# Attention maxima of two heads by pairs of 64-row products, taken in groups of four at the batches of value products

## The chip, the cores and the metric

The kernel runs on one core of one Trainium2 chip. The metric is the device time of one execution in microseconds (us). Five engines work side by side, each through its own list of instructions in order: TensorE (PE: matrix products; PEld is its loading of the stationary operand), VectorE (DVE), ScalarE (ACT), GpSimd (POOL), and SyncE (SP), which issues most DMAs. Products land in PSUM, eight banks of 128 rows by 512 numbers; only DVE and ACT read it here.

## The reference

One layer of a hybrid block over 2048 latent and 256 context tokens. Its first half has two parts that the kernel runs at the same time:

```
s = jnp.einsum('bqkgd,bnkd->bkgqn', q, keys) * scale     # 8 query heads, 2 key heads, head size 64
p = jax.nn.softmax(s, axis=-1)                           # over 2304 keys
o = jnp.einsum('bkgqn,bnkd->bqkgd', p, vals)
...
S_new = exp(b_last) * S + (k * exp(b_last - b))^T v      # gated recurrence, 4 heads, both directions
o = A v + (q * exp(b)) S                                 # A: masked, decayed scores within a chunk
```

Before it come norms and one wide input projection; after it come an output projection and a gated feed-forward layer. The change touches the attention, and two lines of the preparation of its keys.

## The kernel before

**The attention stage.** The work is cut into 32 items: one key head (2) and 128 queries (16), which is four query heads of 128 columns side by side. An item has 18 steps `k`, one for each 128 keys. In a step, `scores` makes one bank `s` of 128 keys by 512 columns with two products (L1190, L1191), and ACT takes its exponential into `p` (L1194). Twice in an item the value products of the steps so far are made in a **batch**: `products` (L1215) and the row sums (L1223). `EVENTS = [10, 20]`: the first batch of an item (eight steps, `av`) is at its own step 10, the second (ten steps) at step 2 of the next item.

**The operands.** A key is kept as a high and a low part of 64 rows each; a tile `K` holds the high parts in rows 0 to 63 and the low parts in rows 64 to 127, and `qa` holds the high part of the queries twice, so that a product over 128 rows adds both parts of the key. `qb` and `KB` (L1191) add the low part of the queries, and take off a maximum.

**The maxima.** The exponential needs, for each query, a bound close to its largest score, before the item starts. So an earlier pass makes the scores the other way round (queries in rows) and keeps only their minimum (signs are turned). `chunk(c)` does a piece: for c under 16, one head and 512 keys (L1159), whose bank `mx` DVE reduces to one column of `mn` (L1161); c = 16 and 17 take the last 256 keys of two heads each (L1165, L1167). After the last one DVE makes `neg` (L1171). At step 10, `maxima` turns it with a transpose `pn` (L1176) and sends it into a row of `qb`. The list `CHUNKS` puts one chunk on each of 18 steps, from step 8 of the item before the last to step 7 of the item before.

**The recurrence** is woven in between. At each batch there is a *round*: products `pa` (L818) for up to two lanes, then `level`, where DVE writes them under a mask into `A` (the copies, L831, one for each lane), ACT moves and POOL multiplies. Transposes `pk` (L889), state products `psf` and `psb` (L902, L922), diagonals `pd` (L804) and readouts `po` (L963 to L965) stand at steps that the tables `KEYS`, `FWD`, `CHAIN`, `DIAG` and `OUT` give; the pattern repeats with each recurrence head, every seven items. `extend` makes the decays `T` on DVE (L873), and the chain of states is carried on DVE from `psb` and `psf` (L943, L915). At step 13 of each item, `finish` makes `pb` (L1239) and DVE scales the item before by it (`oo`, L1241).

**Banks.** PSUM is shared out as `s` 3 banks, `av` 1, `mx` (and `pn`) 2, and `h` 2 for all products of the recurrence and `pb`.

**Order.** In this stage PE, DVE, ACT and POOL each run their instructions in the order in which the program issues them (`manual_schedule`); nothing is moved by a scheduler. In the main loop a step issues its scores, its chunk, work put off by `later`, the recurrence's `step`, `maxima`, `finish`, and at a batch: `pa`, the one sum that DVE adds (L1205), the value products, then `level`.

Of the kernel before, what the change touches and what calls it, by code (L numbers as in the profile page):

```python
# [16 lines left out]
P = 128  # L17
# [19 lines left out]
MLAG = 4  # L37
WL = 1, 3
P5M = False
WOV = (1, 3, 5, 7)  # L40
N_NT = 4
N_S, N_T, N_H = 2, 2, 2
# [25 lines left out]
def block_kernel(ctx: ExitStack, tc: tile.TileContext, a: dict, out: bass.AP, dbg=None):  # L68
# [240 lines left out]
    with proj as st:  # L309
# [223 lines left out]
        def qk_side(t, c):  # L533


            isq = c is not None
            name = f"{'q' if isq else 'k'}{c}_{t}"
            nh = 4 if isq else 2
            n = nh * 64
            lt = t - 2 if t >= 2 else None  # L540
            e = qp.tile([P, 512], F32, tag="qe", name=f"e{name}", bufs=QE)
            raw = e[:, n:2 * n]
            src = s_qraw[c, lt * P:(lt + 1) * P, :] if isq else s_kraw[t * P:(t + 1) * P, :]
            nc.sync.dma_start(raw, src)
# [12 lines left out]
            nc.vector.tensor_tensor(x, hv(raw), rs[:, :, None].to_broadcast([P, nh, 64]), op=ALU.mult)  # L557
            nc.vector.tensor_tensor(x, x, gqk[:, 0 if isq else 1, None, :].to_broadcast([P, nh, 64]),
                                    op=ALU.mult)
            if lt is not None:  # L560
                y = hv(raw)
                y5 = raw.rearrange("p (h g s d) -> p h g s d", g=2, s=2, d=16)
                x5 = e[:, :n].rearrange("p (h g s d) -> p h g s d", g=2, s=2, d=16)
                sn = cs[:, 1, :].rearrange("p (g s d) -> p g s d", g=2, s=2)
                for g in range(2):
                    for s in range(2):
                        nc.vector.tensor_tensor(
                            y5[:, :, g, s, :], x5[:, :, g, 1 - s, :],
                            sn[:, g, s, :][:, None, :].to_broadcast([P, nh, 16]), op=ALU.mult)
# [143 lines left out]
    with ExitStack() as st:  # L713
# [281 lines left out]
        class Recurrence:  # L995
# [112 lines left out]
            def round(self):  # L1108
# [16 lines left out]
                            later(*p[i])  # L1125
                yield

        BATCHES = [[0, 8], [8, 18]]
        ROUNDS = [0, 1]
        EVENTS = [10, 20]  # L1130

        class Item:
# [17 lines left out]

            def chunk(self, c):

                if c == 0:
                    self.mn = sm.tile([P, 4, 5], F32, tag="mn", name=f"mn{self.nm}")
                s = ps_mx.tile([P, 512], F32, tag="x", name=f"mx{self.nm}_{c}")
                K = KS[self.g]
                if c < 16:
                    h, k = divmod(c, 4)
                    nc.tensor.matmul(s, self.qa[:, h * P:(h + 1) * P], K[:, k * 512:(k + 1) * 512],  # L1159
# [2 lines left out]
                else:  # L1162
                    h = (c - 16) * 2
                    for i in range(2):
# [4 lines left out]
                if c == 17:  # L1169
                    self.neg = sm.tile([P, 4], F32, tag="neg", name=f"neg{self.nm}")  # L1170
                    nc.vector.tensor_reduce(self.neg, self.mn, axis=AX.X, op=ALU.min)  # L1171

            def maxima(self):

                pm = ps_mx.tile([P, 512], F32, tag="x", name=f"pn{self.nm}")
                nc.tensor.transpose(pm[:4, :P], self.neg, ident)  # L1176
                mr = sm.tile([4, P], F32R, tag="mr", name=f"mr{self.nm}", bufs=2)
                nc.scalar.activation(mr, pm[:4, :P], AF.Copy)
                for h in range(4):
                    nc.sync.dma_start(f32v(self.qb[64:65, h * P:(h + 1) * P]), f32v(mr[h:h + 1, :]))  # L1180

            def scores(self, k):
# [7 lines left out]
                nc.tensor.matmul(s, KS[self.g][:, ks], self.qa, start=True, stop=False)  # L1190
                nc.tensor.matmul(s, KB[k // 6][:, k % 6 * P:(k % 6 + 1) * P], self.qb,  # L1191
# [55 lines left out]
        KB = [kvp.tile([P, NTOK // 3], F32R, name=f"KB{r}") for r in range(3)]  # L1247
        VS = [kvp.tile([P, 6, 64], F32, name=f"VS{r}") for r in range(3)]
        QB = [qpl.tile([P, 512], F32R, name=f"qb{i}") for i in range(2)]
        one32 = kvp.tile([P, 32], F32, name="one32")  # L1250
        nc.gpsimd.memset(one32, 1.0)
        pick = kvp.tile([P, 2, P], F32, name="pick")
# [8 lines left out]
            nc.sync.dma_start(VS[r], s_v[r * 768:(r + 1) * 768, g * 64:(g + 1) * 64].rearrange("(t p) v -> p t v", p=P))  # L1261

        def load_kb(g, r):
            n = NTOK // 3
            nc.sync.dma_start(f32v(KB[r][:64, :]), s_k[g][:64, r * n:(r + 1) * n])

        for t in QB:
            nc.gpsimd.memset(f32v(t[64:, :]), 0.0)
# [60 lines left out]
        def turn_heads(t, hs, eng, lag=0, ps=ps_h, tag="h"):  # L1329

            pt = ps.tile([P, 512], F32, tag=tag, name=f"mt{t}_{hs[0]}")
            for i, h in enumerate(hs):
                nc.tensor.transpose(pt[:, i * P:(i + 1) * P], mixed[t][0][:, 512 + h * P:512 + (h + 1) * P], ident)
            later(lag, split_mix, t, pt[:, :len(hs) * P], 4 + hs[0], 5 + hs[-1], eng)

        def turn_first():

            turn_heads(FIRST, [0, 1, 2], nc.vector, 1, ps_mx, "x")
            split_mix(FIRST, mixed[FIRST][0][:, :512], 0, 4, nc.gpsimd)

        def load_mix(t):
# [38 lines left out]
        extra[X0].insert(3, (load_att, (FIRST, f32v(KS[0][:, :D]))))  # L1380
        extra[X0].insert(4, (load_heads, (FIRST, range(NH - 1))))
        extra.setdefault(X0 + 10, []).append((turn_first, ()))
        CHUNKS = [-10, -9, -8, -7, -6, -5, -4, -3, -2, -1, 0, 1, 2, 3, 4, 5, 6, 7]
        chunks, loads = {}, {}
        for n in range(1, NIT):
            for c in range(18):
                chunks.setdefault(NKT * (n - 1) + CHUNKS[c], []).append((n, c))

        rec = Recurrence()
        border = ExitStack()  # L1390
# [9 lines left out]
        nc.sync.dma_start(mask, a["k_mask"])  # L1400
        for r in range(3):
            load_v(0, r)
        for x in range(CHUNKS[0], 0):
            for n, c in chunks.pop(x, ()):
                items[n].chunk(c)

        for x in range(NKT * NIT + 1):
            now[0] = x
# [61 lines left out]
            item.scores(k)  # L1470
            if k == 3 and n:
                items[n - 1].drain()
            for m, c in chunks.pop(x, ()):
                items[m].chunk(c)
            for f, args in todo.pop(x, []) + extra.pop(x, []):
                f(*args)
            if k == 5 and n:
# [10 lines left out]
            for e, t in enumerate(EVENTS):  # L1488
# [5 lines left out]
                for p in range(BATCHES[e][0] // 2, BATCHES[e][1] // 2):  # L1494
                    if SUMS[p] in "EQ":
                        items[m].add(p)
                items[m].products(e)
                next(made, 0)
                for ahead, u in rec.decays(x) if e == TE else ():
                    u.extend(min(ahead, 7))  # L1500
                if TE == 9 and e in ROUNDS:
                    for u in rec.lanes.values():
                        u.extend(u.lv)

# [699 lines left out]
```

## Time and profile before

Three runs took 3116.70, 3113.12 and 3107.45 us; the median is 3113.12 us. The profile is of one more execution, which took 3117.9 us, 3116.1 us of it from the first to the last instruction.

| | us |
|---|---|
| profiled execution, and its span | 3117.9, 3116.1 |
| busy in the span: PE | 3074.8 |
| busy in the span: DVE | 1845.9 |
| busy in the span: ACT | 1303.1 |
| busy in the span: POOL | 1602.7 |
| attention stage, about 727 to 1627 us | 900 |

A row of a group names the line, the engine, the operation, what it writes and reads with sizes, the count, the busy time and the mean of one, then the idle time of the engine before it and what ended that. A row of the timeline is start, length, engine, line, operation. A row of the chain of waits is start, length and the instruction that held the end back there. A row of the waits is who waited for whom, with the total in us, the times, and the longest.

### The profile page before, as it was taken

The numbers are of one execution on the slowest core, as the hardware profiler recorded it, in microseconds if no ns is written. First come the engines' busy times: TensorE is split into PE (matmuls) and PEld (weight loads), VectorE is DVE, ScalarE is ACT, GpSimd is POOL, SyncE is SP. The second block draws the span as 40 slices with busy tenths as digits, with TensorE's granted clock in tenths as the row PEclk, the third lists the DMA queues.
The fourth block names the chain that finished last, engine by engine and source line by source line (L and its number), as shares of the span: only waits on it lengthen the run. The fifth ranks groups of instructions, "written<-read, shape, count | busy, mean of one in ns | idle before, by whom it ended". The sixth has DMA issues, their size and how long they took to land.

```text
span 3116.1 us, 51235 instructions
## 1 busy us (share of the span) xinstructions
PE 3074.8 (99%) x18844; PEld 2483.8 (80%) x18844; DVE 1845.9 (59%) x3252; ACT 1303.1 (42%) x2656; POOL 1602.7 (51%) x1291
## 2 busy tenths in 40 slices
PE   9999999999999999999999999999999999999999
PEld 7888888886777778777778878788888788888887
DVE  4554655427777787786745574544478743333567
ACT  4422322214545545555553253333345533333454
POOL 3311212106989888898862118676600277776122
PEclk9999999999999999999999999999999999999999
DMA  7544544425111212111124444656596533333765
GB/s 244 159 139 127 155 139 150 141 69 138 42 38 49 67 53 71 39 52 48 42 83 147 129 142 155 213 176 211 171 331 196 182 118 106 102 102 102 254 195 196
DMA packets 372998, 410.77 MB, mean 132 GB/s; under 512 B 34469, under 2 KB 264073, under 8 KB 372234
## 3 DMA queue, kind: packets, MB, share of 16 engines
q1 hardware_dynamic: 369722, 405.06, 41.0%
q8 instruction: 148, 2.42, 0.3%
q10 hardware_dynamic: 3024, 2.43, 0.2%
q14 instruction: 104, 0.85, 0.1%
HBM read 277.54 MB, written 133.97 MB: 132 GB/s over the span
## 4 chain that ended last, share of the span: by engine, by line
PE 70%; DVE 7%; DMA 5%; POOL 3%; issue 2%; ACT 1%; SPq 1%; POOLq 0%; DVEq 0%; ACTq 0%
PE pA L1785 13%; PE av L1215 7%; PE pB L1785 6%; PE y L1355 6%; PE pd0A L2082 4%; PE pd1A L2082 3%; PE s L1190 3%; PE s L1191 3%; PE pC L1785 3%; PE mx L1159 3%; PE i L442 2%; DVE mn L1161 2%; PE pd0B L2082 2%; PE pd1B L2082 2%; PE pa L818 2%
## 5 line engine op out<-in xcount | busy, mean ns | idle before, releaser
L1194 ACT ACTIVATE p<-s 128x512 f32<-128x512 f32 x576 | 338.2, 600 | 372.6 <-PE s L1191 358.1
L1161 DVE TENSOR_REDUCE mn<-mx 128x1 f32<-128x512 f32 x496 | 337.0, 689 | 175.2 <-PE mx L1159 172.3
L1215 PE MATMUL av<-p,VS 128*64 128x256 f32 x2304 | 259.9, 379 | 0.0
L1190 PE MATMUL s<-qa,K 128*128 128x512 f32 x576 | 244.1, 424 | 1.2 <-ACT p L1194 1.0
L1191 PE MATMUL s<-qb,KB 128*128 128x512 f32 x576 | 226.9, 394 | 0.0
L1215 PEld LDWEIGHTS av<-p,VS 128*64 128x64 f32 x2304 | 160.4, 137 | 75.3 <-issue 1.1
L1205 POOL TENSOR_TENSOR ps<-p,p 128x1024 f32<-128x1024 f32 x64 | 153.4, 2396 | 101.8 <-ACT p L1194 101.7
L1159 PE MATMUL mx<-K,qa 128*128 128x512 f32 x496 | 200.1, 404 | 2.4 <-DVE mn L1161 1.2
L435 PE MATMUL f<-hTh,wh 128*128 128x512 f32 (+1 forms) x640 | 188.1, 373 | 0.2 <-ACT ft L475 0.2
L1205 POOL TENSOR_TENSOR ps<-ps,p 128x1024 f32<-128x1024 f32 x64 | 153.1, 2392 | 12.0 <-ACT p L1194 10.6
L2019 DVE TENSOR_TENSOR dl<-dl,x 128x512 fp32r<-128x512 f32 x154 | 113.8, 765 | 66.5 <-ACT x L2012 64.9
L2012 ACT ACTIVATE x<-dl 128x512 fp32r<-128x512 f32 x154 | 95.9, 631 | 95.4 <-DMA dl<-s_hid0S 37.7
L852 POOL TENSOR_TENSOR Q<-Q,T 128x512 f32<-128x512 f32 x96 | 131.3, 1383 | 8.1 <-PE pa L818 7.7
L435 PEld LDWEIGHTS f<-hTh,wh 128*128 128x128 f32 x640 | 116.9, 190 | 20.4 <-ACT ft L475 0.3
L1190 PEld LDWEIGHTS s<-qa,K 128*128 128x128 f32 x576 | 109.0, 189 | 27.0 <-issue 12.3
L2012 ACT ACTIVATE dh<-dl 128x512 fp32r<-128x512 f32 x154 | 88.9, 624 | 98.7 <-PE pd1A L2082 42.2
L2019 DVE TENSOR_TENSOR dl<-dl,dh 128x512 fp32r<-128x512 f32 x154 | 105.5, 697 | 39.9 <-ACT dh L2012 37.7
L1159 PEld LDWEIGHTS mx<-K,qa 128*128 128x128 f32 x496 | 93.6, 189 | 38.0 <-DVE mn L1161 15.3
L131 POOL TENSOR_TENSOR rs_xf<-ms_xf,mhalf 128x1 f32<-128x1 f32 x16 | 9.9, 620 | 221.1 <-DVE ms_xf L129 218.5
L1191 PEld LDWEIGHTS s<-qb,KB 128*128 128x128 f32 x576 | 109.3, 190 | 14.9
L435 PE MATMUL f<-hTl,wh 128*128 128x512 f32 (+1 forms) x320 | 118.7, 371 | 0.0
L131 POOL TENSOR_TENSOR rs_qq<-ms_qq,mhalf 128x4 f32<-128x4 f32 x32 | 34.0, 1061 | 161.0 <-DVE ms_qq L129 160.3
(436 smaller groups left out, 8913.5 us busy)
## 6 DMA issues: line engine op xcount, KB each, us to landing
w<-in_w_gu_dram SPq DMA_DIRECT2D x88, 512.0 KB
wm<-in_w_mod_dram SPq DMA_DIRECT2D x24, 1024.0 KB
dl<-s_wT SPq DMA_DIRECT2D x88, 256.0 KB
dl<-s_wB SPq DMA_DIRECT2D x66, 256.0 KB
wq<-in_w_down_dram SPq DMA_DIRECT2D x44, 256.0 KB
s_wT<-wq SPq DMA_DIRECT2D x44, 256.0 KB
dl<-s_hid1S SPq DMA_DIRECT2D x44, 256.0 KB
dl<-s_hid0S SPq DMA_DIRECT2D x44, 256.0 KB
```

What stands on the lines that cost most here:

```text
L435: nc.tensor.matmul(pm[:, :n], w[wi][:, k, c0:c0 + P], hT[b][hi][:, k, :], start=(k == 0 and i == 0), stop=(k == KT - 1 and i == 2))
L1159: nc.tensor.matmul(s, self.qa[:, h * P:(h + 1) * P], K[:, k * 512:(k + 1) * 512], start=True, stop=True)
L1161: nc.vector.tensor_reduce(self.mn[:, h, k:k + 1], s, axis=AX.X, op=ALU.min)
L1190: nc.tensor.matmul(s, KS[self.g][:, ks], self.qa, start=True, stop=False)
L1191: nc.tensor.matmul(s, KB[k // 6][:, k % 6 * P:(k % 6 + 1) * P], self.qb, start=False, stop=True)
L1194: nc.scalar.activation(self.pairs[p][:, o:o + 512], s, AF.Exp, scale=-1.0)
L1205: (nc.gpsimd if SUMS[p] in "PQ" else nc.vector).tensor_tensor(t, a, self.pairs[p], op=ALU.add)
L1215: nc.tensor.matmul(self.av[i * 64:(i + 1) * 64, :256], VS[k // 6][:, k % 6, :], self.pairs[k // 2][:, o:o + 256], start=(k == 0), stop=(k ...
L1355: nc.tensor.matmul(py, m[:, k, :], wo[k][w][hf], start=(k == 0 and i == 0), stop=(k == KT - 1 and i == 2), skip_group_check=True)
L1785: nc.tensor.matmul(acc, w[wi][:, k, :], x[xi][k], start=(start and k == 0 and i == 0), stop=(stop and k == KH - 1 and i == 2), skip_group_ ...
L2019: nc.vector.tensor_tensor(lo, f32v(lo), f32v(hi), op=ALU.subtract)
L2082: nc.tensor.matmul(cur[t], l[:, t * P:(t + 1) * P], r, start=(start and j == 0 and f == 0), stop=(stop and j == NHF - 1 and f == 2), skip_ ...
```

## The change

Heads 0 and 1 of an item lose their eight chunks of 128 rows. In their place `chunk(0)` and `chunk(1)` make a head each by four products of 64 rows, high part of the key alone, into four banks: two take rows 0 to 63, two take rows 64 to 127, in turn. For this the high and the low part of a key change places in every second group of four tiles (`flipped`), so that 512 consecutive keys have their high parts in the lower rows and the next 512 in the upper; `load_kb`, which needs the high parts in rows 0 to 63, takes two or three DMAs for each third in place of one. DVE reduces the four banks one after another, and these four reductions are issued in front of the round's `level`, that is, of the copies into `A`. The two groups stand behind the value products of the batches, at step 10 and step 2. The other ten chunks stand at steps 13 to 17, 0, 1, and 5 to 7. The banks of `s` and of `mx` are taken in turn as one ring of five (`bank`). `neg` becomes a fixed tile of 128 columns that is turned whole, and is made a step after the last chunk.

```diff
+def flipped(t):
+    return t // 4 % 2 if t < 16 else t % 2
...
-                nc.scalar.activation(sk[:, :, 0, :], x, AF.Copy)
-                nc.vector.tensor_tensor(sk[:, :, 1, :], x, f32v(sk[:, :, 0, :]), op=ALU.subtract)
+                f = flipped(t)
+                nc.scalar.activation(sk[:, :, f, :], x, AF.Copy)
+                nc.vector.tensor_tensor(sk[:, :, 1 - f, :], x, f32v(sk[:, :, f, :]), op=ALU.subtract)
...
+        taken = [0]
+        def bank(name):
+            n = taken[0] = taken[0] + 1
+            pl, tag = ((ps_st, "s"), (ps_mx, "x"))[n % 5 % 2]
+            return pl.tile([P, 512], F32, tag=tag, name=name)
...
-                s = ps_mx.tile([P, 512], F32, tag="x", name=f"mx{self.nm}_{c}")
                 K = KS[self.g]
+                if c < 2:
+                    banks = [bank(f"mx{self.nm}_{c}{i}") for i in range(4)]
+                    for i, s in enumerate(banks):
+                        r = slice(i % 2 * 64, i % 2 * 64 + 64)
+                        nc.tensor.matmul(s, self.qa[r, c * P:(c + 1) * P], K[r, i * 512:(i + 1) * 512],
+                                         start=True, stop=True)
+                    for i, s in enumerate(banks):
+                        nc.vector.tensor_reduce(self.mn[:, c, i:i + 1], s, axis=AX.X, op=ALU.min)
+                    return
+                s = bank(f"mx{self.nm}_{c}")
...
-                s = ps_st.tile([P, 512], F32, tag="s", name=f"s{nm}")
+                s = bank(f"s{nm}")
...
-        CHUNKS = [-10, -9, -8, -7, -6, -5, -4, -3, -2, -1, 0, 1, 2, 3, 4, 5, 6, 7]
+        CHUNKS = [(-8, 0), (2, 1)] + list(zip((-5, -4, -3, -2, -1, 0, 1, 5, 6, 7), range(8, 18)))
+        FIRST_CHUNKS = [(-1, c) for c in range(8, 17)] + [(2, 0), (6, 1), (7, 17)]
...
                 items[m].products(e)
+                for i, c in chunks.pop(x, ()):
+                    items[i].chunk(c)
                 next(made, 0)
```

DVE behind a batch at step 2, where no carry of the recurrence stands. `A_` are the targets of the copies, `T_` the decays, `mn_` the minima. Before:

```order
L831 COPY_PREDICATED A_10928<-mask,pa_11189 128x512
L831 COPY_PREDICATED A_10107<-mask,pa_11189 128x512
L873 TENSOR_REDUCE T_5_11255<-T_4_11098 128x16
L873 TENSOR_REDUCE T_1_11257<-T_0_11100 128x256
L1161 TENSOR_REDUCE mn_0_10992<-mx_0_13_11267 128x1
L1161 TENSOR_REDUCE mn_0_10992<-mx_0_14_11276 128x1
L1161 TENSOR_REDUCE mn_0_10992<-mx_0_15_11283 128x1
L1167 TENSOR_REDUCE mn_0_10992<-mx_0_16_11298 128x2
L1167 TENSOR_REDUCE mn_0_10992<-mx_0_17_11307 128x2
L1171 TENSOR_REDUCE neg_0_11311<-mn_0_10992 128x4
```

With the change (L1177 reduces the group's four banks, and the last digit of their names is the bank; L1184 and L1190 are single chunks):

```order
L1177 TENSOR_REDUCE mn_0_11070<-mx_0_10_11231 128x1
L1177 TENSOR_REDUCE mn_0_11070<-mx_0_11_11232 128x1
L1177 TENSOR_REDUCE mn_0_11070<-mx_0_12_11233 128x1
L1177 TENSOR_REDUCE mn_0_11070<-mx_0_13_11234 128x1
L837 COPY_PREDICATED A_10926<-mask,pa_11177 128x512
L837 COPY_PREDICATED A_10104<-mask,pa_11177 128x512
L879 TENSOR_REDUCE T_5_11255<-T_4_11095 128x16
L879 TENSOR_REDUCE T_1_11257<-T_0_11097 128x256
L1184 TENSOR_REDUCE mn_0_11070<-mx_0_15_11277 128x1
L1190 TENSOR_REDUCE mn_0_11070<-mx_0_16_11292 128x2
L1190 TENSOR_REDUCE mn_0_11070<-mx_0_17_11301 128x2
L1197 TENSOR_REDUCE neg<-mn_0_11070 128x4
```

The copies and the decays moved from ahead of the first reduction after the batch to behind four reductions.

PE behind a batch at step 2 where a readout `po` stands at step 3 (`s_1_3` is the score of step 3, `av` the last row sums). Before:

```order
L1223 MATMUL av_1_12730<-p_1_8_12856,one_7125 32x128 x8
L1190 MATMUL s_1_3_12994<-qa_1_12264,K_7116 128x512
L1191 MATMUL s_1_3_12994<-qb_7124,KB_7117 128x512
L1159 MATMUL mx_1_13_13002<-K_7116,qa_1_12617 128x512
L963 MATMUL po_13011<-V_9556,A_10928 128x128
L964 MATMUL po_13011<-S_10997,Q_10929 128x128
L965 MATMUL po_13011<-Sb_11_12797,Q_10929 128x128
```

With the change:

```order
L1249 MATMUL av_1_12713<-p_1_8_12846,one_7127 32x128 x8
L1174 MATMUL mx_1_10_12965<-K_7116,qa_1_12611 128x512
L1174 MATMUL mx_1_11_12966<-K_7116,qa_1_12611 128x512
L1174 MATMUL mx_1_12_12967<-K_7116,qa_1_12611 128x512
L1174 MATMUL mx_1_13_12968<-K_7116,qa_1_12611 128x512
L1216 MATMUL s_1_3_12993<-qa_1_12255,K_7116 128x512
L1217 MATMUL s_1_3_12993<-qb_7124,KB_7117 128x512
L969 MATMUL po_13007<-V_9551,A_10926 128x128
L970 MATMUL po_13007<-S_10987,Q_10927 128x128
L971 MATMUL po_13007<-Sb_11_12787,Q_10927 128x128
```

The four products of the group came in between the row sums and the score of step 3, the chunk between that score and the readout went, and the readout still writes into the bank that the round's `pa` had, from which DVE copies.

More of the change, by code (lines that the diff above doesn't have):

```diff
@@ L1168, in chunk, with lowest @@
                                             axis=AX.X, op=ALU.min)
-                if c == 17:
-                    self.neg = sm.tile([P, 4], F32, tag="neg", name=f"neg{self.nm}")
-                    nc.vector.tensor_reduce(self.neg, self.mn, axis=AX.X, op=ALU.min)
+                if c == LAST_CHUNK:
+                    later(1, self.lowest)
+            def lowest(self):
+                nc.vector.tensor_reduce(neg_all[:, :4], self.mn, axis=AX.X, op=ALU.min)
             def maxima(self):
-                pm = ps_mx.tile([P, 512], F32, tag="x", name=f"pn{self.nm}")
-                nc.tensor.transpose(pm[:4, :P], self.neg, ident)
+                pm = bank(f"pn{self.nm}")
+                nc.tensor.transpose(pm[:, :P], neg_all, ident)
                 mr = sm.tile([4, P], F32R, tag="mr", name=f"mr{self.nm}", bufs=2)
@@ L1249, in block_kernel @@
         QB = [qpl.tile([P, 512], F32R, name=f"qb{i}") for i in range(2)]
+        neg_all = kvp.tile([P, P], F32, name="neg")
+        nc.gpsimd.memset(neg_all, 0.0)
         one32 = kvp.tile([P, 32], F32, name="one32")
@@ L1263, in load_kb @@
         def load_kb(g, r):
-            n = NTOK // 3
-            nc.sync.dma_start(f32v(KB[r][:64, :]), s_k[g][:64, r * n:(r + 1) * n])
+            t0 = 6 * r
+            while t0 < 6 * r + 6:
+                t1 = t0
+                while t1 < 6 * r + 6 and flipped(t1) == flipped(t0):
+                    t1 += 1
+                rows = slice(64 * flipped(t0), 64 * flipped(t0) + 64)
+                nc.sync.dma_start(f32v(KB[r][:64, (t0 - 6 * r) * P:(t1 - 6 * r) * P]), s_k[g][rows, t0 * P:t1 * P])
+                t0 = t1
         for t in QB:
@@ L1336, in turn_first @@
         def turn_first():
-            turn_heads(FIRST, [0, 1, 2], nc.vector, 1, ps_mx, "x")
+            turn_heads(FIRST, [0, 1, 2], nc.vector, 1, bank(f"mt{FIRST}_0"))
             split_mix(FIRST, mixed[FIRST][0][:, :512], 0, 4, nc.gpsimd)
@@ L1402, in block_kernel @@
             load_v(0, r)
-        for x in range(CHUNKS[0], 0):
+        for x in range(-1, 0):
+            now[0] = x
             for n, c in chunks.pop(x, ()):
                 items[n].chunk(c)
+            for f, args in todo.pop(x, []):
+                f(*args)
         for x in range(NKT * NIT + 1):
@@ L1472, in block_kernel @@
                 items[n - 1].drain()
-            for m, c in chunks.pop(x, ()):
-                items[m].chunk(c)
+            if k not in (2, 10):
+                for m, c in chunks.pop(x, ()):
+                    items[m].chunk(c)
             for f, args in todo.pop(x, []) + extra.pop(x, []):
@@ L1503, in block_kernel @@
                         u.extend(u.lv)
+            for m, c in chunks.pop(x, ()):
+                items[m].chunk(c)
     with ExitStack() as st:
```

12 lines of the change are left out of this document (7 added, 5 removed).

## The prediction

> **What bounds the kernel now.** I read the page's first part, then the stage in which the change lies, cut into stretches, then the chain of waits there, and last DVE's timeline beside it.
>
> ```profile
> PE 3074.8 (99%) x18844; PEld 2483.8 (80%) x18844; DVE 1845.9 (59%) x3252; ACT 1303.1 (42%) x2656; POOL 1602.7 (51%) x1291
> ```
>
> ```profile
> 727.00:1627.00 900.00, 892.79 (x8418) 681.59 (x8416) 672.51 (x1087) 475.15 (x1078) 776.70 (x618) 1.00 0.20 56
> ```
>
> ```profile
> 1283.45:1290.34 6.89, 6.89 (x106) 5.01 (x106) 4.85 (x9) 1.13 (x3) 6.75 (x6) 1.00 0.12 32
> 1290.34:1296.20 5.86, 5.76 (x27) 4.33 (x26) 5.07 (x9) 4.81 (x9) 4.24 (x2) 1.00 0.31 92
> 1301.40:1308.90 7.50, 7.50 (x38) 5.97 (x34) 6.38 (x10) 5.45 (x10) 7.42 (x7) 1.00 0.17 46
> ```
>
> The first row says that PE is the bound: 99% busy. The columns of the others are the stretch, then PE, PEld, DVE, ACT, POOL, the granted clock (1.00), and DMA. In the attention stage PE has 893 of 900 us and DVE only 673. But an average hides where DVE is free. The three short stretches are a batch, and the steps behind two batches: among the steps DVE has 5.07 of 5.86 us and 6.38 of 7.50.
>
> ```profile
> 1284.81 4.32 PE av L1215 x40
> 1290.14 0.43 PE s L1190
> 1290.56 0.23 PE s L1191
> 1291.07 1.38 DVE mn L1161 x2
> 1294.59 0.17 DVE neg L1171
> 1296.29 1.12 PE pa L818 x32
> 1297.40 3.46 PE av L1215 x32
> 1303.71 0.45 PE pb L1239 x4
> 1309.04 1.08 PE pa L818 x32
> ```
>
> ```profile
> 1284.51 0.68 DVE L1161 TENSOR_REDUCE mn<-mx 128x1 f32<-128x512 f32 x1
> 1285.11 1.80 DVE L1205 TENSOR_TENSOR ps<-ps,p 128x1024 f32<-128x1024 f32 x1
> 1286.84 1.38 DVE L831 COPY_PREDICATED A<-mask,pa 128x512 f32<-128x512 int32 x2
> 1288.11 0.27 DVE L873 TENSOR_REDUCE T<-T 128x64 f32<-128x128 f32 x1
> 1291.07 2.08 DVE L1161 TENSOR_REDUCE mn<-mx 128x1 f32<-128x512 f32 x3 [2.70 <-PE mx L1159]
> 1299.17 1.36 DVE L831 COPY_PREDICATED A<-mask,pa 128x512 f32<-128x512 int32 x2
> 1300.43 0.79 DVE L873 TENSOR_REDUCE T<-T 128x32 f32<-128x64 f32 x2
> 1304.36 0.41 DVE L1241 TENSOR_TENSOR oo<-ot,pb 128x256 f32<-128x256 f32 x1
> ```
>
> The chain is already held by DVE's reductions from 1291.07 to the transpose before the products `pa` at 1296.29, in a stretch in which the recurrence adds nothing. And DVE's free time lies under the value products: its sum, its two copies and a decay run from 1285.11 to 1288.38, and then it waits 2.70 us for the first reduction. That window is the one thing which the copies lose here: they go from under the value products to behind four reductions that can only start after them.
>
> **The change on PE.** Before, each of the eight chunks is one product.
>
> ```profile
> 1290.07 0.50 PE L1190 MATMUL s<-qa,K 128*128 128x512 f32 x1
> 1290.40 0.40 PE L1191 MATMUL s<-qb,KB 128*128 128x512 f32 x1
> 1290.64 0.40 PE L1159 MATMUL mx<-K,qa 128*128 128x512 f32 x1
> ...
> 1296.22 1.19 PE L818 MATMUL pa<-Q,M 128*64 128x64 f32 x32
> ...
> 1301.37 0.50 PE L1190 MATMUL s<-qa,K 128*128 128x512 f32 x1
> ```
>
> ```profile
> 1191.45 0.89 PE psb L922 x8
> ...
> 1223.81 0.22 PE pk L889 x2
> ...
> 1405.54 0.23 PE po L963 x2
> 1408.00 0.22 PE po L965 x2
> ```
>
> From start to start a product of 512 columns takes 0.23 us (1290.40 to 1290.64), eight take 1.84. Does a pair of 64 rows run side by side? No row of before shows products split by rows. The nearest split by columns: a 128-column f32 product `po` takes 0.22, so a 256-column one 0.44 and sixteen 7.0, yet the sixteen `av` of an eight-step batch, two halves of the columns in turn, take 3.46. So halves overlap fully there. Bounds for a pair are 0.23 and 0.46; I take 0.23, since `av` is the nearest. By the Trainium skill, TensorE: Matmul & The Clock Gate, section "Measured speedup vs the span model", tiles of one size take one product's time and about 4 ns more for each further tile, which would make a pair 0.234 us and leave the sum as it is.
>
> Against this stands a change of the array's split. The first score behind the row sums (32 columns wide) takes 0.43 on the chain, and the next product 0.23: 0.20 for going back to the full array. A group stands between the two, so I charge it a second 0.20; the bounds are 0 (hidden) and 0.40 (both directions dearer by half rows). A rule of the skill speaks against the change here too: TensorEngine Tiling (Array Packing), section "Key Properties", says that changing the mode drains TensorE; by it 0.20 is paid at each group, and without it nothing. The sum on PE for an item: 8 x 0.23 - 4 x 0.23 - 2 x 0.20 = 0.52 us saved, 16 us over 31 items; 28 without the second 0.20. That is all that the change can give.
>
> **The change on DVE.** The number of reductions, 18 an item, stays, and so does a reduction's price: 0.60 us from one to the next (1284.51 to 1285.11). I walk a stretch without recurrence, counting from the start of the first product behind a batch (T). The first product behind a batch takes 0.50, and DVE begins 0.03 after a product's end (1290.64 + 0.40 against 1291.07), so the four reductions start at 0.53, 1.13, 1.73, 2.33 and the copies at 2.93. The copies end at 4.29 (1.36), the decays start at 4.19 (1299.17 to 1300.43 is 1.26) and take 0.27 to 0.79, of which 0.08 overlaps what follows: DVE is free for the next chunk at 4.45 to 4.9. PE meanwhile: the group 0.43 + 0.23, the change back 0.20, so the first score starts at 0.86, and each score takes 0.46.
>
> *Steps 3 to 10.* Three chunks are left (5, 6, 7) and `neg`: 3 x 0.60 + 0.09 + 0.17 = 2.06, so `neg` is done at 6.5 to 6.95, and `pa` starts 0.2 later, after the transpose: 6.7 to 7.15. PE alone would be there at 0.86 + 8 x 0.46 + 3 x 0.23 + 0.2 = 5.4. Before, from 1290.07 to 1296.22, 6.15. So **0.55 to 1.0 slower, I take 0.8**.
>
> *Steps 11 to 2.* Seven chunks (13 to 17, 0, 1) and `oo`. The score of step 2 takes the bank of the chunk five places before it, the fifth of the seven, so it waits for 5 x 0.60 + 0.41 + 0.09: 7.95 to 8.4, `pa` 0.46 later at 8.4 to 8.9. Before, 1301.37 to 1309.04: 7.65, with `pb` at 0.45 inside. So **0.75 to 1.2 slower, I take 1.0**. The group's wait for `s` of steps 12 and 13, whose banks are the group's first two, is short: reduced at 1.22 and 1.83, wanted at 1.32 and 1.78.
>
> *Where the recurrence has products in the stretch* PE has work to fill these gaps, and would gain 0.5 in steps 3 to 10 (one group for four chunks, of eight) and about nothing in 11 to 2 (one group and seven chunks for ten). But the copies free the bank of `pa` only at 4.35, and in the built program the next product which takes it waits there:
>
> ```profile
> 1400.86 1.36 DVE L831 COPY_PREDICATED A<-mask,pa 128x512 f32<-128x512 int32 x2
> ```
>
> Before, that copy ended at 1402.22 and the readout in its bank began at 1405.54: no wait. With the change the readout of step 3 would be ready at T + 1.3 and starts at 4.35: 3.0 lost, less the 0.5, 2.5 in three items. By the same walk, with a pair of `pk` at 0.22, four at 0.45, and `psb` at 0.89: a second `pk` at step 5, ready at 2.9, +0.9 (four items); `psf` at step 6, ready at 4.06, -0.2 (four); `pb` at step 13 behind a `pk`, ready at 2.9, +1.4 (four); a readout at step 13, ready at 3.3, +1.1 (three); `pb` behind a `psb`, ready at 3.4, and the readout of step 14 behind DVE's carries, +1.5 (three); `pb` with no product of the recurrence after it, ready at 2.6, so that 7 scores and 6 chunks (4.6) end at 9.4 against 7.65: +1.8 (four); `pk` at 15 and 16, +0.3 (four). What waits behind each on PE is the next score, so the exponentials and POOL's sums move with it; POOL is busy 777 of 900 us; longer stretches give it more room.
>
> **The sum.** By the tables of the recurrence, 19 of 31 stretches from step 3 and 11 of 30 from step 11 are of the plain kind: 19 x 0.8 + 11 x 1.0 = 26. The others: 3 x 2.5 + 4 x 0.9 - 4 x 0.2 + 4 x 1.4 + 3 x 1.1 + 3 x 1.5 + 4 x 1.8 + 4 x 0.3 = 32. Together 58 us. The ring of five costs nothing by itself where DVE keeps up; where it doesn't, its cost is in the walk. The split of the keys changes no size on ACT and DVE; four more DMAs for each key head lie in SP's queue far ahead of their use; the turned `neg` is the same 0.11 product. I count these as nothing; uncovered, the DMAs would be a few us once. The profiled execution took 3117.9, so 3176; it lies 4.8 above the median of the runs, so I predict **3171**.
>
> **Rivals.**
> *Faster: DVE's lateness is absorbed.* DVE has 227 us free in the stage. If it runs the four reductions and the copies without PE coming to wait (a reduction faster on a bank that nobody else writes, or waits that fall into gaps I took for full), PE's saving stands: 3113 - 16 = 3097, 3085 if the second change of split is free. It decides if a walk ends before PE does, at T + 5.4 instead of 6.5. For it: DVE's 75%. Against it: the 2.70 us of idleness sits where the copies were, and the chain already runs through DVE.
> *Only half the waits.* DVE is late as walked, but the copies' bank costs nothing (another bank is free, or the products come later): 26 us, less 0.5 in the other 12 stretches from step 3: +20, 3133.
> *The pairs don't overlap.* The change then doesn't do what it says. Each group takes 0.92 for 0.46. Where DVE holds the stretch this is covered; in the other 31 it costs up to 0.46, 14 us: 3185.
> *A wash.* The late copies hurt in the plain stretches and the rest gains from more freedom in the ring: within 9 us of 3113.
>
> **How the numbers follow.** The forecast 0.53, with its own range 3145 to 3190; half the waits 0.15; no overlap 0.07; a wash 0.10; faster 0.15. A difference counts from 0.3%, 9 us: faster 0.15, same 0.10, slower 0.75. The range leaves out most of the faster case and what lies above no overlap: 3100 to 3195.
>
> **What would show it.** PE's busy time in the stage should fall, and gaps should stand in front of it: at the score of step 2, `<-DVE` from reductions, at `pn` from `neg`, and at `po`, `pb`, `pk` from the copies. DVE should run without a gap from the group to `pa`, with its idle time moved under the value products. Starts of the pair's two products close together, and 0.2 between the pairs, would show the overlap. The forecast is wrong if the score of step 12 or `pn` waits for nothing, or if DVE has idle time between the group and the next batch.

## The result and the profile after

The changed kernel takes 3190.4 us (median of five runs, 3182.5 to 3193.6) against 3113.3 us: **slower, ratio 1.0246, 95% interval 1.0228 to 1.0264**, 77 us. The forecast was 3171, in a range of 3100 to 3195. The profiled execution took 3182.5 us. Of all executions reported below a single one, of the ring alone, stands apart at 8701 us, with PE's products two to three times as long throughout; why stays open, and it is left out of the ratio.

The first part of the page and the attention stage (columns as in the prediction):

```profile
PE 3095.2 (97%) x18844; PEld 2447.5 (77%) x18844; DVE 1811.7 (57%) x3252; ACT 1300.7 (41%) x2656; POOL 1598.8 (50%) x1292
```

```profile
727.00:1690.00 963.00, 906.29 (x8303) 640.21 (x8302) 631.50 (x1079) 463.47 (x1061) 760.31 (x613) 0.99 0.17 49
```

PE had 7 us without work in the 900 us of this stage; now it has 57 in 963. Its busy time rose too, from 893 to 906 us, where the prediction had it fall: a score that had to wait for its bank shows 0.50 us where others show 0.40, and in some items the granted clock fell. The waits from 763 to 1680 us say behind whom (who waited for whom: total us, times, longest). After the change L1174 are the group's products and L1177 its reductions, L1182 and L1184 a single chunk, L1216 a score, L837 the copies, L879 the decays.

```profile
...
DVE mn L1177 <- PE mx L1174: 231.0, 57, 5.5
...
PEld s L1216 <- DVE mn L1177: 37.3, 107, 0.7
...
PE s L1216 <- DVE mn L1184: 11.5, 18, 1.6
...
PE po L969 <- DVE T L879: 9.1, 3, 3.0
...
```

And further down, among the waits of PE alone:

```profile
PE pb L1265 <- DVE T L879: 6.0, 4, 1.6
PE pk L895 <- DVE A L837: 5.8, 5, 1.3
...
PE pb L1265 <- DVE A L837: 4.5, 4, 1.2
```

DVE stands idle 57 times, up to 5.5 us, for the group's first product, with its copies queued behind; then scores wait for DVE's reductions, and readouts, `pb` and `pk` wait for the copies' bank (the profile names the decay, which DVE runs last before). A plain stretch from step 11 to 2, first on PE, then on DVE:

```profile
1113.81 3.62 PE L1241 MATMUL av<-p,VS 128*64 128x256 f32 x32
1117.36 0.64 PE L1249 MATMUL av<-ps,one 128*32 128x128 f32 x16
1117.93 0.73 PE L1174 MATMUL mx<-K,qa 64*128 64x512 f32 x4
1118.60 0.50 PE L1216 MATMUL s<-qa,K 128*128 128x512 f32 x1
1118.93 0.40 PE L1217 MATMUL s<-qb,KB 128*128 128x512 f32 x1
1119.21 0.50 PE L1216 MATMUL s<-qa,K 128*128 128x512 f32 x1
...
1119.81 0.50 PE L1216 MATMUL s<-qa,K 128*128 128x512 f32 x1
...
1124.52 0.50 PE L1216 MATMUL s<-qa,K 128*128 128x512 f32 x1 [0.82 <-DVE mn L1184]
...
1127.27 1.15 PE L824 MATMUL pa<-Q,M 128*64 128x64 f32 x32
```

```profile
1118.47 2.48 DVE L1177 TENSOR_REDUCE mn<-mx 128x1 f32<-128x512 f32 x4 [3.49 <-PE mx L1174]
1120.87 1.39 DVE L837 COPY_PREDICATED A<-mask,pa 128x512 f32<-128x512 int32 x2
1122.12 0.81 DVE L879 TENSOR_REDUCE T<-T 128x32 f32<-128x64 f32 x2
1122.84 0.69 DVE L1184 TENSOR_REDUCE mn<-mx 128x1 f32<-128x512 f32 x1
1123.43 0.42 DVE L1267 TENSOR_TENSOR oo<-ot,pb 128x256 f32<-128x256 f32 x1
1123.76 3.85 DVE L1184 TENSOR_REDUCE mn<-mx 128x1 f32<-128x512 f32 x6
1127.52 1.22 DVE L1231 TENSOR_TENSOR ps<-ps,p 128x1024 f32<-128x1024 f32 x1
```

DVE is idle under the value products and then has no gap from the group to behind `pa`. The four reductions stand 0.60 apart, and so do the first scores, which want 0.46. In what follows a *stretch* runs from the start of one batch's value products to the start of the next, "from step 3" or "from step 11" by the step behind the batch. Summed over the 31 stretches of each kind, those from step 3 are 34 us longer than before, those from step 11 46 us. The window of 963 us above is too short to show these 80: from the first value product to the last the changed kernel takes 980.0 us (716.3 to 1696.3), the kernel before 901.4 (726.2 to 1627.6).

### The profile page after: what moved, and what is told of

Read it like the earlier page. It is cut to its first block, busy times and chain, and to the rows that moved or that the text cites. A ratio compares the mean times of both kernels' runs of the same rounds, so it can differ in the third digit from the quotient of the medians.

```text
span 3180.7 us, 51294 instructions
## 1 busy us (share of the span) xinstructions
PE 3095.2 (97%) x18844; PEld 2447.5 (77%) x18844; DVE 1811.7 (57%) x3252; ACT 1300.7 (41%) x2656; POOL 1598.8 (50%) x1292
## 4 chain that ended last, share of the span: by engine, by line
PE 51%; DVE 3%; ACT 1%; issue 1%; POOL 0%; DMA 0%; SPq 0%; POOLq 0%; ACTq 0%; DVEq 0%
PE pA L1830 15%; PE pB L1830 7%; PE y L1390 5%; PE pd0A L2127 4%; PE pC L1830 4%; PE pd1A L2127 3%; PE av L1241 2%; PE pd0B L2127 2%; PE pd1B L2127 2%; PE pd0C L2127 1%; PE pd1C L2127 1%; PE s L1216 1%; DVE mn L1177 1%; PE s L1217 1%; PE pa L824 0%
## 5 line engine op out<-in xcount | busy, mean ns | idle before, releaser
L1177 DVE TENSOR_REDUCE mn<-mx 128x1 f32<-128x512 f32 x248 | 154.1, 684 | 238.3 <-PE mx L1174 238.2
L1216 PE MATMUL s<-qa,K 128*128 128x512 f32 x576 | 262.6, 456 | 21.7 <-DVE mn L1184 12.5
L1231 POOL TENSOR_TENSOR ps<-p,p 128x1024 f32<-128x1024 f32 x64 | 153.1, 2392 | 135.2 <-ACT p L1220 134.7
L1216 PEld LDWEIGHTS s<-qa,K 128*128 128x128 f32 x576 | 108.9, 189 | 109.3 <-DVE mn L1177 40.1
L1184 DVE TENSOR_REDUCE mn<-mx 128x1 f32<-128x512 f32 x248 | 164.3, 688 | 27.7 <-PE mx L1182 27.2
L1231 POOL TENSOR_TENSOR ps<-ps,p 128x1024 f32<-128x1024 f32 x64 | 152.7, 2386 | 17.3 <-ACT p L1220 16.0
L858 POOL TENSOR_TENSOR Q<-Q,T 128x512 f32<-128x512 f32 x96 | 119.2, 1257 | 29.3 <-PE pa L824 29.3
L2094 POOL TENSOR_TENSOR y<-y,yg 128x512 f32<-128x512 f32 x24 | 40.6, 1706 | 144.8 <-DVE yg L2093 142.9
L1830 PE MATMUL pB<-x,S1h 128*128 128x512 f32 x352 | 109.8, 393 | 3.4 <-ACT S1h L1799 3.4
```

The source lines that it names most:

```text
L1177: nc.vector.tensor_reduce(self.mn[:, c, i:i + 1], s, axis=AX.X, op=ALU.min)
L1184: nc.vector.tensor_reduce(self.mn[:, h, k:k + 1], s, axis=AX.X, op=ALU.min)
L1231: (nc.gpsimd if SUMS[p] in "PQ" else nc.vector).tensor_tensor(t, a, self.pairs[p], op=ALU.add)
L1830: nc.tensor.matmul(acc, w[wi][:, k, :], x[xi][k], start=(start and k == 0 and i == 0), stop=(stop and k == KH - 1 and i == 2), skip_group_ ...
```

## The experiments

In the expectations and below, the *held sum* is the one sum of exponentials that DVE adds at a batch (`ps`, L1231). All times are medians beside runs of the kernel before on the same chip (3111.7 in the first set, 3112.8 and 3112.7 in the others).

| run | us | ratio to before, interval |
|---|---|---|
| group behind the copies | 3114.2 | 1.0008, 0.9999 to 1.0017 |
| the same, full products | 3118.3 | 1.0022, 1.0011 to 1.0032 |
| the change, full products | 3189.2 | 1.0248, 1.0232 to 1.0263 |
| ring alone | 3101.8 | 0.9968, 0.9956 to 0.9981 |
| ring alone, again | 3101.8 | 0.9966, 0.9953 to 0.9979 |
| group in front of the value products | 3129.2 | 1.0057, 1.0038 to 1.0075 |
| the same, reductions last | 3128.1 | 1.0047, 1.0032 to 1.0062 |
| the same as in front, full products | 3138.2 | 1.0081, 1.0063 to 1.0099 |
| one group in front, one behind | 3111.5 | 0.9997, 0.9987 to 1.0006 |
| one group in front, no other | 3111.3 | 0.9996, 0.9986 to 1.0005 |

**Is it the order on DVE?** The theory is the prediction's: the copies and decays that now stand between the group and the next chunk. The rivals are the burst of reductions itself, the pairs, and the ring. The first run moves the group behind the round's `level`:

```diff
                 items[m].products(e)
-                for i, c in chunks.pop(x, ()):
-                    items[i].chunk(c)
                 next(made, 0)
                 for ahead, u in rec.decays(x) if e == TE else ():
                     u.extend(min(ahead, 7))
...
+                for i, c in chunks.pop(x, ()):
+                    items[i].chunk(c)
```

> The changed kernel with one thing moved: at the batch VectorE gets the round's two copies and the decays first and the group's four reductions behind them, so the copies can run under the value products again. Pairs, groups and ring stay. Theory (the copies and the decays between the group and the next chunk are what the change costs): DVE is free for the next chunk at T + 2.93 instead of 4.45 to 4.9, the copies' bank is free before the value products end; the steps 3 to 10 come down to PE's 5.4 to 5.8 between first product and pa, the steps 11 to 2 to 7.5 to 8; the time goes back to 3095 to 3125 us, and the waits PE po, pk, pb <- DVE copies vanish. Rival (the burst of four reductions, paced at 0.60 against a score's 0.46 in a ring of five, is the cost, wherever the copies are): at least 3150. Rival (half and half): 3130 to 3150.

Measured: 3114.2 us. The place of the group on one engine's list is worth 1.0246 against 1.0008, about 74 us, and that is the whole loss against the kernel before. The waits of `po`, `pb` and `pk` for the copies are gone from the list. A plain stretch from step 3, DVE and then PE:

```profile
1099.98 1.36 DVE L837 COPY_PREDICATED A<-mask,pa 128x512 f32<-128x512 int32 x2
1101.22 0.52 DVE L879 TENSOR_REDUCE T<-T 128x16 f32<-128x32 f32 x2
1105.26 2.48 DVE L1177 TENSOR_REDUCE mn<-mx 128x1 f32<-128x512 f32 x4 [3.53 <-PE mx L1174]
1107.66 0.68 DVE L1184 TENSOR_REDUCE mn<-mx 128x1 f32<-128x512 f32 x1
```

```profile
1104.73 0.73 PE L1174 MATMUL mx<-K,qa 64*128 64x512 f32 x4
1105.39 0.50 PE L1216 MATMUL s<-qa,K 128*128 128x512 f32 x1
...
1106.01 0.50 PE L1216 MATMUL s<-qa,K 128*128 128x512 f32 x1
...
1106.61 0.50 PE L1216 MATMUL s<-qa,K 128*128 128x512 f32 x1
...
1107.80 0.50 PE L1216 MATMUL s<-qa,K 128*128 128x512 f32 x1 [0.23 <-DVE mn L1177]
...
1110.89 1.15 PE L824 MATMUL pa<-Q,M 128*64 128x64 f32 x32
```

The copies are back under the value products, and the next chunk is reduced at 1107.66, 2.93 us behind the group's start, to the hundredth as walked. But `pa` comes at 6.16, not at 5.4 to 5.8: the score at 1107.80 stands three scores and a chunk behind the one at 1105.39, 1.61 by their pitches, and comes after 2.41. Of the missing 0.80, 0.10 is the first product behind the group (0.34 to the next start, for 0.24), and the rest is the burst: scores take banks that are given back every 0.60 us. So the rival mechanism is there too; it just eats what PE saves rather than making the kernel slower.

**Do the pairs overlap, and is that worth anything?** In three places the pairs were made full products, in the changed kernel first:

```diff
-                        nc.tensor.matmul(s, self.qa[r, c * P:(c + 1) * P], K[r, i * 512:(i + 1) * 512],
+                        nc.tensor.matmul(s, self.qa[:, c * P:(c + 1) * P], K[:, i * 512:(i + 1) * 512],
```

> The changed kernel with the group's four 64-row products made as full 128-row products (the same order, banks and reductions). Theory (the pairs overlap and save about 0.25 us a group on PE, but VectorE's chain from the group's first product decides in the plain stretches): 3190 to 3206, with 0.92 instead of 0.67 us from the group's start to the next score. Rival (the pairs don't overlap, or their change of the array's split costs as much as they save): 3180 to 3190, the same or faster.

```profile
1110.91 1.21 PE L1174 MATMUL mx<-K,qa 128*128 128x512 f32 x4
1111.96 0.40 PE L1216 MATMUL s<-qa,K 128*128 128x512 f32 x1
1112.20 0.39 PE L1217 MATMUL s<-qb,KB 128*128 128x512 f32 x1
```

Measured: 3189.2, no difference, which is the number of the rival and not its reason. In the trace the products of a pair start 0.003 us apart: they overlap. From the group's start to the next score four full products take 1.05 us, the two pairs 0.67 (1117.93 to 1118.60 above). But behind pairs the first product of that score takes 0.33 to the next start (1118.60 to 1118.93), behind full products 0.24 (1111.96 to 1112.20). Counted up to that second product, the median of the 62 groups is 1.26 us with full products and 1.00 with pairs: the pairs save 0.26 us a group, 16 us in all. None of it reaches the time, because DVE holds the stretch. With the group behind the copies:

> Group behind the copies on VectorE, as in the run before with that order, and full 128-row products in the group: what is left of the change is that four chunks stand together at each batch, and the ring. Theory: without VectorE's lateness PE decides, so the full products cost 0.25 us x 62 groups = up to 15 us over the run with pairs in that order: 3105 to 3140. Rival (reductions still pace the stretch): within 4 us of the run with pairs.

Measured: 3118.3, 4 us above the run with pairs, of the 16 that PE saves. The intervals of the two runs just overlap, so this is at the edge between theory and rival; what paces the stretch there is mostly DVE's 0.60.

**What does the ring do by itself?**

```diff
-                s = ps_mx.tile([P, 512], F32, tag="x", name=f"mx{self.nm}_{c}")
+                s = bank(f"mx{self.nm}_{c}")
...
-                s = ps_st.tile([P, 512], F32, tag="s", name=f"s{nm}")
+                s = bank(f"s{nm}")
```

> The kernel before with one thing added: scores, chunks and the turned maxima take their banks in turn out of the ring of five, in place of three for scores and two for chunks. One chunk a step, full products, copies as before. Theory (the ring alone costs nothing where VectorE keeps up): 3107 to 3120. Rival (the ring ties scores to reductions and costs by itself): over 3125.

> The kernel before with the ring of five alone, once more, to see where its time goes. Theory now (two banks for the chunks made PE wait for a reduction where chunks stand close, as before the first scores and in the recurrence's stretches; five in a ring let it run on): 3098 to 3106, the gain mostly at the start of the attention. Rival (the gain is spread over every step's weight loads): the same time, but each stretch 0.1 to 0.2 shorter.

Measured: 3101.8 both times. Neither theory of the first run had it: the ring alone makes the kernel **faster than both**, by 0.3%. The waits of the kernel before, from 763 to 1600 us, show what it removes:

```profile
PEld mx L1159 <- DVE mn L1161: 9.6, 34, 0.6
...
PEld pn L1176 <- DVE mn L1161: 8.0, 20, 0.4
```

With two banks for chunks, a weight load for a chunk, or for the turned maxima, often waited for a reduction. With the ring the second line is gone, and in place of the first there are 4.2 us for exponentials and, in front of scores, 5.2 for reductions. That these shorter waits are what the ring gains is argued, not shown. A plain stretch from step 3 takes 12.22 us for 12.55, from step 11 12.62 for 12.72. From the first score to the last value product it is 905.4 us for 910.8. The first value products also come 7.5 us earlier, but that can't be counted: PE is 5.8 us ahead when the projections end, before the ring is used, and in the profile of before the first chunks and scores ran at half clock (columns as above):

```profile
712.40:719.30 6.90, 6.58 (x12) 3.82 (x13) 5.40 (x8) 0.74 (x2) 0.00 (x0) 0.53 1.09 268
```

So of the 11 us between the medians, 5.4 can be placed, and they are the spread-out gain of the second expectation's rival, though not in each stretch: 0.33 in the plain ones from step 3, 0.10 from step 11, and two from step 3 grow by 0.8.

**Can the reductions go under the value products?** If a burst 0.60 apart must stand somewhere, DVE's free time is under the value products. The group was put between `pa` and them:

```diff
                 next(made, 0)
+                for i, c in chunks.pop(x, ()):
+                    items[i].chunk(c)
                 for p in range(BATCHES[e][0] // 2, BATCHES[e][1] // 2):
```

> The changed kernel with the group moved in front of the value products (behind pa): its four reductions run under the value products, ahead of the held sum, the copies and the decays, which all still fit there. Theory (what is left of the loss in the run with the group behind the copies is that four reductions 0.60 apart stand between scores 0.46 apart: 0.8 us a batch of scores waiting for banks, which eats the 0.6 that PE saves in steps 3 to 10): with the reductions under the value products no score waits, steps 3 to 10 are 0.6 shorter than before, steps 11 to 2 as long as before; 3114 - 31 x 0.6 - 30 x 0.3 = 3086, range 3075 to 3100, and faster than both kernels. Rival (the held sum, now behind four reductions, ends after the value products and PE waits in front of the row sums instead): 3105 to 3130, with a wait of av for ps. Rival (the group waits for the exponentials of the last scores, since it needs four banks at once there): 3100 to 3120, with a wait mx <- ACT p.

```profile
1097.74 2.48 DVE L1177 TENSOR_REDUCE mn<-mx 128x1 f32<-128x512 f32 x4 [1.29 <-PE mx L1174]
1100.14 2.33 DVE L1231 TENSOR_TENSOR ps<-ps,p 128x1024 f32<-128x1024 f32 x1
```

```profile
1097.87 3.67 PE L1241 MATMUL av<-p,VS 128*64 128x256 f32 x32
1102.52 0.64 PE L1249 MATMUL av<-ps,one 128*32 128x128 f32 x16 [0.98 <-DVE ps L1231]
```

```profile
PE av L1249 <- DVE ps L1231: 27.0, 29, 3.3
```

Measured: 3129.2, the first rival. Scores hardly wait any more, and plain stretches from step 3 are 0.6 shorter than before, as expected. But the held sum, which now starts 2.40 us later, ends after the value products, and PE waits in front of the row sums: 27 us in 29 places, 23 of them batches of 32 products. The obvious repair, reductions last:

> The group's products in front of the value products as in the run with that place, but VectorE takes the held sum, the copies and the decays first, and the four reductions last. Theory: the reductions then end 5.9 us after the value products' start, when scores have begun: the third and fourth bank come 0.2 to 0.5 late in the 32-product batches, nothing in the 40-product ones; 0 to 20 us above the run with the reductions first. Rival (the held sum late behind the reductions is what costs): 0 to 20 us below it.

```profile
PE mx L1174 <- ACT p L1221: 12.7, 4, 3.8
```

Measured: 3128.1, the same, by another wait. The plain items are now the shortest of all runs (24.7 us for the two stretches, 25.3 before), and the wait for the held sum is gone. But in the stretches where ACT itself waits for POOL the group stands in front of the value products and waits for banks that the last exponentials have not left: 12.7 us in four places, in front of everything on PE. The pairs' worth in this place:

> The run with the group in front of the value products, with full 128-row products in the group. Here nothing of VectorE covers the group, so this prices the pairs: theory (two pairs save 0.46 on PE, less one change of the array's split, 0.2): 0.25 x 62 = 15 us above that run. Rival (the changes of split eat it): within 5 us. If each pair saved its whole 0.23 and changes were free: 28 us above.

Measured: 3138.2, 9 us above the run with pairs: between the two numbers, 0.15 us a group. But the premise does not hold, something of DVE does cover the group. By starts two pairs save 0.46 us here (medians of 0.93 and 1.39, up to the second pair of value products), 28 us in all; yet PE then waits for the held sum for 27.0 us, with full products for 7.0. Those 20 us are waited away again, which leaves about the 9 that were measured.

**Each group at its better place, or only one of them.**

> The changed kernel with each of the two groups at the place where it was cheaper: at the batch of step 2 (40 value products) in front of the value products, reductions ahead of the held sum; at the batch of step 10 (32 products) behind the value products, with the copies and decays ahead of the reductions. Theory (places are independent of each other): stretches from step 3 as in the run with the group in front (0.6 below before in the plain ones), stretches from step 11 as in the run with the group behind (0.3 above before): 3114 - 19 = 3095, range 3088 to 3106. Rival (the stretches hang together through POOL's sums and the exponentials, and what one gains the next gives back): 3106 to 3120.

> Only the group of step 2 is left, in front of the value products; the other head's chunks are full products, one a step, so that 14 single chunks and one group stand in place of 18. Theory (a group saves 0.1 to 0.25 us of PE where its reductions are hidden, and what stands above the ring alone in the other runs is the group of step 10): 3092 to 3104, within 6 us of the ring alone (3102). Rival (groups cost by themselves wherever they stand): 3107 to 3120.

Measured: 3111.5 and 3111.3, both equal to before within the interval and 10 us above the ring alone; both times the rival's range. The estimate of the first was booked wrongly: a group in front of the value products lies in the stretch before it, one behind in the stretch after, so both groups fell into the stretch from step 11 (39 us more than before in all), and none into that from step 3 (35 less). The two effects that were added had been measured with one group in each. In the second a plain item takes 24.82 us, the ring alone 24.84: there a group of two pairs in front of the value products costs as much as the four single chunks that it replaces. Against the ring alone all stretches from step 11, which hold the group, are 20.1 us longer, and those from step 3, which have three chunks fewer, 10.9 shorter. Of these, 10.8 are in the plain ones: where the recurrence has products, taking the chunks out saves nothing in sum. Why was not settled. The largest single piece is 1.6 us in each of three stretches in which the group waits up to 0.9 for an exponential.

## Why the prediction was right, and where its sizes were off

**PE's saving is small: right.** It was put at 0.52 us an item, 0.26 a group, and by starts it is 0.26 a group. The second 0.20 that was charged at each group for the change of split has the right size, but by luck. It was read off the chain of waits (0.43 against 0.23), and from start to start that same score takes 0.33 (1290.07 to 1290.40): one change costs 0.10, not 0.20. The rest of the 0.20 stands elsewhere: the group's second pair and the first product behind it take 0.33 each from start to start, for 0.23. Since DVE decides, the time would not have shown a wrong size.

**The DVE walk: right.** Walked from T: reductions at 0.53, copies at 2.93, decays at 4.19, next chunk at 4.45 to 4.9. In the stretch shown (T = 1117.93): 0.54, 2.94, 4.19, 4.91.

**Plain stretches from step 3: right.** 0.8 was taken; 17 of them grew by 0.76 on average, eleven by 0.57 to 0.94, four by 1.1 to 1.2 and two by nothing. `neg` was done 6.4 to 7.0 behind the group's start (walked: 6.5 to 6.95). The sign to look for was a gap at `pn`; there are few (3.4 us, 7 times, in front of its weight load), because in about half of these stretches a score in front of `pn` had already waited for a reduction of the same chain.

**Plain stretches from step 11: too small.** 1.0 was taken, 1.6 to 1.9 is usual (15.6 us in ten of them). The step that failed is the choice of the score that waits. The score of step 2 was taken to wait for the fifth chunk, at 7.95 to 8.4. The one that waits is that of step 17, at 1124.52 (T + 6.59), for the second single chunk, reduced at 1123.76 + 0.68. From there PE still has three scores with their chunks, 0.70 each, and one more score of 0.46, which makes T + 9.15; `pa` started at T + 9.34, not at 8.4 to 8.9. The walk looked at the end of DVE's chain and not at what PE has left to do behind each of its links.

**Stretches with the recurrence: right in kind, one of them half the size.** Readouts at step 3: the walk had them start 3.0 late, and all three do (3.03, 3.02, 3.02). The first stretch grew by 2.9, against the 2.5 taken, but the other two by 5.7 and 4.6:

```profile
1233.20 0.77 PE L969 MATMUL po<-V,A 128*128 128x128 f32 x2 [3.02 <-DVE T L879]
1233.76 0.63 PE L970 MATMUL po<-S,Q 128*128 128x128 f32 x2
```

```profile
1233.10:1238.30 5.20, 5.10 (x24) 5.13 (x25) 1.59 (x5) 0.00 (x0) 0.14 (x1) 0.50 0.01 3
```

There the granted clock fell to 0.50 during the wait and stayed there, and products that take 0.39 took 0.63. `pb` alone behind the batch was taken at +1.8 and is +2.7 to +3.1, by the same error as in the plain stretches; a second `pk` at step 5 +0.9 taken, +1.1 measured; `pb` behind `pk` +1.4 and +1.6; readout at step 13 +1.1 and +1.2; `pb` behind `psb` +1.5 and +1.45; `pk` at 15 and 16 +0.3 and +0.7; `psf` at step 6, -0.2 taken, came out anywhere from -0.3 to +1.5.

**The sum: near, and partly by luck.** The stretches grew by 80 us, and the sum had 58. The plain ones from step 11 (5 us), the readouts at step 3 (6) and `pb` alone (4) make most of the difference. Without the ring's gain, which the sum put at nothing, it would have been some 10 us larger; that part is luck.

**"The ring of five costs nothing by itself": wrong in sign.** It gains 10 us. With the ring counted, the other parts cost some 87 us, of which the order on DVE is 74.

**The rivals.** The faster one was that DVE's lateness is absorbed. It fails on the order, and even with the order mended the burst takes what PE saves. That the pairs don't overlap is refuted. "Only half the waits" is refuted by the waits for the copies' bank. A wash had one thing right: the ring does gain.

## What to carry to other kernels

On an engine that runs its list in order, an instruction that must wait for a late product holds back everything behind it: put first what can start now, here the copies, and the same group of instructions costs 0.1%, which is not clear of nothing, instead of 2.5%. When work is gathered into a burst, compare the pace at which the consumer gives banks back (0.60) with the pace at which the next producer takes them (0.46), and walk every link of the ring with what the producer has left behind it, not only the last. And test the helpers of a change alone: the shared ring of banks, brought in to make room for the groups, was the one part that made the kernel faster.

## What was not expected of the hardware

**Short waits of PE can cost a second time.** Three waits of 3.03, 3.02 and 3.02 us, in front of the same products in three items, were followed by different clocks:

```profile
1010.00:1014.00 4.00, 4.00 (x30) 3.59 (x28) 1.18 (x4) 2.10 (x7) 1.29 (x1) 1.00 0.00 0
```

This is behind the wait that ended at 1008.92: the clock stayed at 1.00. In the wait that ended at 1233.20 it fell to 0.50 at 1232.48 and stayed there for 6.83 us. Behind the third, which ended at 1460.62, it fell at 1461.17 for 3.41 us, and once more at 1290.50 for 3.41 us, behind a wait of 1.44. These falls are 17 and 50 times 3.413 us apart, so they sit on one fixed grid. In the steps of that grid just before them PE was idle for 2.31, 2.86 and 1.44 us; the wait that cost nothing is cut by the grid into 1.31 and 1.72. No threshold comes out of these few rows, but they fit a cost that depends on how the grid cuts a wait. Against the same stretch in other items the three concerned are 2.8, 1.6 and 0.4 us longer. The Trainium skill, TensorE: Matmul & The Clock Gate, section "Part 1: The HAM clock gate", has the clock fall to half after an idle window of about 3.4 us that runs freely, so that the same kernel can fare differently. The length and the free running agree with these rows; they also show that PE need not be idle for the whole window.

**The held sum on DVE has no fixed price.** The same addition of 128 x 1024 took 1.17 us at one batch and 6.15 at another of the same execution (the ring alone):

```profile
1149.11 6.15 DVE L1213 TENSOR_TENSOR ps<-ps,p 128x1024 f32<-128x1024 f32 x1
...
1168.06 1.17 DVE L1213 TENSOR_TENSOR ps<-ps,p 128x1024 f32<-128x1024 f32 x1
```

The long one lies beside seven of POOL's multiplications (`M`, `Q` and `C`). The short one lies beside one, which itself took 1.32 us where the same one took 0.41 a little before, at 1167.30; so the two engines seem to hold each other up, but no run tested it. For the group in front it mattered: with 1.22, as at 1127.52 above, and not 2.33 the held sum would have ended with the value products.
